# Giving out the last head's second attention pass at the hold point of the stream

## The chip, the cores and the metric

The kernel runs on one core of a Trainium2 chip. The metric is the device time of one execution in microseconds (us). A profile of one execution gives, instruction by instruction, when each engine worked and what it waited for: PE (TensorE, with PEld its weight loads), DVE (VectorE), ACT (ScalarE), POOL (GpSimd) and SP (SyncE, which issues nearly all DMAs here, in order).

## The reference

One layer of a streaming encoder over 2048 positions, 1024 wide, in float32:

```
h   = RMSNorm(x);  z = h @ W_in
A   = gMLP heads:   u * (W_s LN(v) + b), in blocks of 128 positions
B   = 8 FoX heads:  softmax(q k^T / sqrt(64) + c[t] - c[s]) v,  s <= t,
                    c = cumsum(log sigmoid(forget logits))
x   = x + concat(A, B) @ W_out
x   = x + ConvFFN(RMSNorm(x))
out = RMSNorm(x)
```

The change concerns B, the attention, and W_out, which reads A and B.

## The kernel before, in words

Matrix products are made of three matmuls each: operands are split into a rounded high part and the remainder (hi, lo), and mm3 (lines 208, 210 and 212) adds hi hi, hi lo and lo hi. These are the main matmuls; most are 512 wide.

The positions are worked on in two halves of 1024, each of two blocks of 512 (tb = 0 to 3 over both). **Phase A** projects both halves (a_half): gated units, values, keys and queries. **Phase C** (c_half) multiplies the mixed rows by W_out, adds x, and makes the scaled, transposed rows for the ConvFFN. **Phase D** (d_half) is the up-projection of the first half. After it come the second half's C and D and the down-projection.

**The attention stream.** Attention runs beside these phases. b_stream is a generator over 32 pieces (h, tb), in order tb = 0 with heads 0 to 7, then tb = 1, and so on. A piece has two passes. b_max (the first pass) computes the scores of 512 queries against all keys up to them, their running minimum and sums (lines 745 to 754), and from these the row maximum, which a function, turn, transposes on TensorE (line 779) and writes into the tile t1. b_mix (the second pass) recomputes the scores transposed (lines 806 and 807), takes exp (812), splits it into ph and pl (817, 818) and multiplies by the values into the PSUM tile o (794, 795). At a head's end op takes the sum of o's two halves (829, 830); at each odd head op is scaled and split, and written to the DRAM tensors mixh and mixl of that block.

The second pass of a piece is given out after the first pass of the next piece, and that next piece's turn is called inside it, after three of its steps. So todo holds one piece whose second pass is still to come. After every main matmul tick counts, and after each 3.5 to 4.4 of them (RATES) one step of the stream is given out, with priority over the main work. The scheduler then orders each engine's instructions.

**The hold.** The pieces of tb = 2 and 3 need keys and queries of the second half, so b_stream does not begin (0, 2) before ready is set, when phase A has ended; until then it yields without giving anything out. In the kernel's text the stream reaches that point 542 ticks before the end of phase A, with todo = (7, 1).

**Who needs (7, 1).** c_half works on block 0 and then on block 1, each in two column groups of four row tiles. Before the second column group of block 0 it calls need(1), which gives out steps until 16 pieces are done, and then load_mix(1), which reads the mixed rows of block 1 from mixh and mixl into the tiles thi and tlo, in four quarters each (k = 0 to 7 in pairs). The last quarter, k = 6 and 7, holds heads 4 to 7. Each finished row tile is written to rows (DMA rows<-acc), and its buffer acc is loaded anew for block 1 (acc<-in_x_dram); GpSimd makes a scaled copy, ar (line 886), whose eight column blocks TensorE transposes into dn. Weights come through raw (DMA), are rounded by GpSimd (whi, line 150) and split by VectorE (wlo, line 162). In phase D GpSimd also subtracts column blocks of w_down in a tile tw (line 967).

Of the kernel before, what the change touches and what calls it, by code (L numbers as in the profile page):

```python
# [80 lines left out]
class Block:  # L81
# [600 lines left out]
    def b_stream(self, pieces):  # L682

        todo = None
        for h, tb in pieces:
            while tb >= 2 and not self.ready:
                yield
            t1, t2, turn = yield from self.b_max(h, tb)
            if todo:
                yield from self.b_mix(*todo, turn)  # L690
                self.done += 1
            else:
                turn()
            todo = (h, tb, t1, t2, self.rr)
        yield from self.b_mix(*todo, None)
        self.done += 1
# [814 lines left out]
```

## Time and profile before

| | |
|---|---|
| median of 3 timed runs | 2437.68 us (2436.88 to 2441.38) |
| span of the profiled execution | 2436.2 us, 1.5 under that median |
| PE busy | 2409.5 us, 99% |
| DVE, ACT, POOL busy | 1755.8, 1348.5 and 312.5 us |
| phase C begins on PE (first main matmul of c_half) | 592.0 us |
| head 7's second pass over block 1 on PE | 649 to 669 us |

The profile is read as follows. A view of stretches gives busy time by engine and the clock that TensorE was granted (1.00 is full). A timeline gives start, length and the instruction as output<-inputs, and in brackets how long the engine was idle just before and what ended that. Matmul ends are modelled and overlap the next start, so the pace is read from starts. SPq is SyncE's queue: the start of a DMA there is when it was issued, not when it landed.

### The profile page before, as it was taken

To read this page: it belongs to the slowest core of one execution; us is meant where nothing else is said; L and a number is where in the kernel's file an instruction comes from. 1 tells how busy PE (TensorE), PEld (TensorE's weight loads), DVE (VectorE), ACT (ScalarE), POOL (GpSimd) and SP (SyncE) were. 2 spreads that over 40 slices of the span, in tenths; PEclk is the share of its full clock that TensorE was granted. 3 is DMA by queue.
4 is the path that set the end of the run, shared out by engine and by line. 5 is a ranking of instruction groups with operands and counts; after the bars stand their busy time and mean duration, and the time that the engine had idled before them with its cause. 6 is when DMAs were issued, how large, how long until landed. Compare 5 with 4: busy or idle time off the path is not lost.

```text
span 2436.2 us, 32591 instructions
## 1 busy us (share of the span) xinstructions
PE 2409.5 (99%) x10984; PEld 1982.9 (81%) x10984; DVE 1755.8 (72%) x3086; ACT 1348.5 (55%) x2635; POOL 312.5 (13%) x303
## 2 busy tenths in 40 slices
PE   9999999999999999999999999999999999999998
PEld 7788888788777888888888888888888888888887
DVE  5448776565557878878778774498888877957775
ACT  4347766544455556667676671365555555454443
POOL 3114140000213221111111201100000000000000
PEclk9999999999999999999999999999999999999999
DMA  8854646658756545554555436312222228538633
GB/s 290 276 140 123 199 120 174 169 170 280 215 158 213 187 154 164 163 166 144 179 175 180 157 123 236 140 56 80 85 87 87 78 92 311 164 99 297 206 115 121
DMA packets 245031, 400.51 MB, mean 164 GB/s; under 512 B 51240, under 2 KB 109736, under 8 KB 243440
## 3 DMA queue, kind: packets, MB, share of 16 engines
q1 hardware_dynamic: 239824, 374.31, 48.3%
q0 software_dynamic: 5040, 24.12, 2.5%
q8 instruction: 87, 1.43, 0.2%
q14 instruction: 80, 0.66, 0.1%
HBM read 304.76 MB, written 93.72 MB: 164 GB/s over the span
## 4 chain that ended last, share of the span: by engine, by line
PE 93%; DMA 3%; DVE 1%; ACT 1%; issue 0%; POOL 0%; SPq 0%; DVEq 0%; POOLq 0%; ACTq 0%
PE D L1351 16%; PE mm L210 14%; PE mm L208 14%; PE mm L212 14%; PE A L1149 3%; PE A L1150 3%; PE A L1151 3%; PE o L795 2%; PE o L794 2%; PE s L746 2%; PE s L745 2%; PE s L807 2%; PE s L806 2%; PE B L1150 2%; PE B L1151 2%; PE B L1149 2%
## 5 line engine op out<-in xcount | busy, mean ns | idle before, releaser
L210 PE MATMUL mm<-tlo,whi 128*128 128x512 f32 x912 | 358.1, 393 | 0.0
L208 PE MATMUL mm<-thi,whi 128*128 128x512 f32 x912 | 357.7, 392 | 0.0
L212 PE MATMUL mm<-thi,wlo 128*128 128x512 f32 x912 | 357.5, 392 | 0.0
L208 PE MATMUL mm<-whi,thi 128*128 128x512 f32 x640 | 252.9, 396 | 2.9 <-DMA thi<-mixh 2.2
L150 POOL TENSOR_SCALAR whi<-raw 128x1024 fp32r<-128x1024 f32 (+1 forms) x112 | 125.9, 1125 | 1005.1 <-PE mm L210 616.8
L210 PE MATMUL mm<-wlo,thi 128*128 128x512 f32 x640 | 251.3, 393 | 0.1
L212 PE MATMUL mm<-whi,tlo 128*128 128x512 f32 x640 | 251.0, 393 | 0.0
L754 ACT ACTIVATE s<-s,part 128x512 f32<-128x512 f32 (+3 forms) x261 | 154.6, 592 | 130.7 <-DVE part L749 81.4
L208 PEld LDWEIGHTS mm<-thi,whi 128*128 128x128 f32 x912 | 171.5, 188 | 35.7
L210 PEld LDWEIGHTS mm<-tlo,whi 128*128 128x128 f32 x912 | 171.5, 188 | 35.5
L212 PEld LDWEIGHTS mm<-thi,wlo 128*128 128x128 f32 x912 | 171.5, 188 | 34.8
L818 DVE TENSOR_TENSOR pl<-e,ph 128x512 fp32r<-128x512 f32 (+2 forms) x212 | 136.9, 655 | 76.8 <-ACT ph L817 39.3
L162 DVE TENSOR_TENSOR wlo<-raw,whi 128x1024 fp32r<-128x1024 f32 x104 | 136.2, 1309 | 54.0 <-POOL whi L150 53.6
L812 ACT ACTIVATE e<-s 128x512 f32<-128x512 f32 (+2 forms) x216 | 110.3, 527 | 95.3 <-DVE s L810 41.0
L208 PEld LDWEIGHTS mm<-whi,thi 128*128 128x128 f32 x640 | 120.6, 188 | 26.9 <-DMA thi<-mixh 2.5
L1351 PE MATMUL D<-wl,xh 128*128 128x512 f32 x368 | 141.3, 389 | 0.0
L1351 PE MATMUL D<-wh,xh 128*128 128x512 f32 x368 | 140.8, 389 | 0.2 <-DVE xo L1429 0.2
L212 PEld LDWEIGHTS mm<-whi,tlo 128*128 128x128 f32 x640 | 120.3, 188 | 24.3 <-DMA tlo<-mixl 0.7
L210 PEld LDWEIGHTS mm<-wlo,thi 128*128 128x128 f32 x640 | 120.6, 188 | 23.5 <-DVE wlo L162 0.5
L817 ACT ACTIVATE ph<-e 128x512 fp32r<-128x512 f32 (+2 forms) x212 | 116.3, 562 | 39.5 <-PE o L794 34.1
L1351 PE MATMUL D<-wh,xl 128*128 128x512 f32 x368 | 137.1, 389 | 0.0
L749 DVE TENSOR_REDUCE part<-s 128x1 f32<-128x512 f32 x149 | 98.2, 683 | 21.4 <-PE s L746 20.7
(1898 smaller groups left out, 5853.7 us busy)
## 6 DMA issues: line engine op xcount, KB each, us to landing
raw<-in_w_up_dram SPq DMA_DIRECT2D x72, 512.0 KB
m<-kx SPq DMA_DIRECT2D x133, 256.0 KB
m<-kx SPq DMA_DIRECT2D x160, 136.0 KB
x<-act SPq DMA_DIRECT2D x84, 256.0 KB
raw<-in_w_in_dram SPq DMA_DIRECT2D x36, 512.0 KB
v<-vd SPq DMA_DIRECT2D x66, 256.0 KB
raw<-in_w_out_dram SPq DMA_DIRECT2D x24, 512.0 KB
tw<-in_w_down_dram SPq DMA_DIRECT2D x11, 1024.0 KB
```

What stands on the lines that cost most here:

```text
L150: self.cast_ins = self.nc.gpsimd.tensor_scalar(out, in_, 1.0, 0.0, ALU.mult, ALU.add).ins
L162: nc.vector.tensor_tensor(lo, raw, f32(hi), op=ALU.subtract)
L208: mm(ps, lhsT=ah[k], rhs=bh[k], start=k == 0, stop=False)
L210: mm(ps, lhsT=ah[k], rhs=bl[k], start=False, stop=False)
L212: self.last_mm = mm(ps, lhsT=al[k], rhs=bh[k], start=False, stop=k == n - 1).ins
L754: nc.scalar.activation(ps[:, :n], ps[:, :n], AF.Exp, scale=-1.0, bias=dst, accum_out=ls[:, tt, sb:sb + 1])
L817: nc.scalar.activation(ph[:, c], e[:, c], AF.Copy)
L818: nc.vector.tensor_tensor(pl[:, c], e[:, c], f32(ph[:, c]), op=ALU.subtract)
L1149: mm(ps, lhsT=xh[:, ks], rhs=yh[:, k, :], start=fresh and k == 0, stop=False, **kw)
L1150: mm(ps, lhsT=xh[:, ks], rhs=yl[:, k, :], start=False, stop=False, **kw)
L1151: mm(ps, lhsT=xl[:, ks], rhs=yh[:, k, :], start=False, stop=k == 3, **kw)
L1351: nc.tensor.matmul(bank[t], lhsT=x[i][:, ts], rhs=w[k], start=fresh and j == 0 and i + k == 0, stop=last and i == 1, **kw)
```

## The change

When the stream comes to a piece that is held back, it now gives out the second pass of the piece before at once, with no turn in it (None), counts it as done and empties todo. Then it waits as before. The held piece's own turn is later called directly after its first pass, as for the stream's first piece.

```
         todo = None
         for h, tb in pieces:
-            while tb >= 2 and not self.ready:
-                yield
+            if tb >= 2 and not self.ready:
+                if todo:
+                    yield from self.b_mix(*todo, None)
+                    self.done += 1
+                    todo = None
+                while not self.ready:
+                    yield
             t1, t2, turn = yield from self.b_max(h, tb)
             if todo:
                 yield from self.b_mix(*todo, turn)
```

Lines behind it are numbered five higher in the changed kernel (794 becomes 799, 806 becomes 811). It also changes what stands on the engines, from the place where head 6's second pass over block 1 ends. Here is TensorE there, in the kernel before: o is head 6's output, mm main work of phase C, and lines 745 and 746 head 0's first pass over block 2.

```order
L795 MATMUL o_1160_4894<-pl_1201_5033,v_1187_4984 128x256
L794 MATMUL o_1160_4894<-ph_1204_5048,v_1187_4984 128x128
L208 MATMUL mm_1443_6373<-whi_1432_6350,thi_1321_5823 128x512
L745 MATMUL s_1359_6022<-m1_53_394,t1_55_396 128x512
L745 MATMUL s_1360_6032<-m1_53_394,t1_55_396 128x512
L745 MATMUL s_1361_6041<-m1_53_394,t1_55_396 128x512
L746 MATMUL s_1359_6022<-m2_1358_6019,t2_1354_6012 128x512
L795 MATMUL o_1160_4894<-pl_1205_5049,v_1187_4984 128x128
```

The same place on TensorE in the changed kernel; lines 811 and 812 are head 7's second pass over block 1.

```order
L799 MATMUL o_1160_4894<-ph_1200_5032,v_1187_4984 128x256
L811 MATMUL s_1210_5077<-t1_54_395,m1_53_394 128x512
L811 MATMUL s_1214_5090<-t1_54_395,m1_53_394 128x512
L811 MATMUL s_1220_5109<-t1_54_395,m1_53_394 128x512
L812 MATMUL s_1214_5090<-t2_1124_4764,m2_1208_5072 128x512
L812 MATMUL s_1210_5077<-t2_1124_4764,m2_1208_5072 128x512
L800 MATMUL o_1160_4894<-pl_1201_5033,v_1187_4984 128x256
L799 MATMUL o_1160_4894<-ph_1204_5048,v_1187_4984 128x128
```

Head 7's second pass now stands where head 0's first pass over block 2 stood, and the latter comes behind it.

SyncE's queue of DMAs, where head 7's result is written (mixh1, mixl1) and the last quarter of block 1 read (thi_1428, tlo_1430), before; qx, kx and vd are queries, keys and values of the stream.

```order
L100 DMA v_1473_6525<-vd0_77 128x4x128
L100 DMA v_1492_6590<-vd0_77 128x4x128
L100 DMA m1_52_393<-kx1_74 68x512
L100 DMA m2_1457_6457<-kx1_74 128x512
L100 DMA mixh1_80<-ph_1420_6317 128x512
L100 DMA thi_1428_6338<-mixh1_80 128x2x512
L100 DMA mixl1_84<-pl_1421_6318 128x512
L100 DMA m1_53_394<-kx0_73 68x512
L100 DMA m2_1472_6522<-kx0_73 128x512
L100 DMA tlo_1430_6340<-mixl1_84 128x2x512
```

The same in the changed kernel (the tiles are thi_1439 and tlo_1441 there).

```order
L100 DMA acc_1563_6795<-in_x_dram 128x1024
L100 DMA v_1487_6540<-vd0_77 128x4x128
L100 DMA m1_53_394<-kx1_74 68x512
L100 DMA m2_1410_6222<-kx1_74 128x512
L100 DMA rows0_3_90<-acc_1381_6102 128x1024
L100 DMA mixh1_80<-ph_1250_5240 128x512
L100 DMA mixl1_84<-pl_1251_5241 128x512
L100 DMA acc_1564_6797<-in_x_dram 128x1024
L100 DMA thi_1439_6389<-mixh1_80 128x2x512
L100 DMA tlo_1441_6391<-mixl1_84 128x2x512
```

Write and read moved forward, in among the last of the four writes of row tiles (rows0) and the loads of acc for block 1; before, all of these stood ahead of them.

GpSimd at the start of phase D before, where ar_1705 is the scaled copy of the last row tile of block 1.

```order
L175 TENSOR_SCALAR rs_1707_7436<-ss_1706_7434 128x1
L150 TENSOR_SCALAR whi_1731_7464<-raw_1730_7463 128x1024
L177 TENSOR_TENSOR rstd_1708_7438<-rs_1707_7436,mhalf_63 128x1
L886 TENSOR_SCALAR ar_1705_7433<-acc_1547_6735,rstd_1708_7438 128x1024
L967 TENSOR_TENSOR tw_1839_7920<-tw_1839_7920 128x512 x2
L150 TENSOR_SCALAR whi_1935_8330<-raw_1934_8329 128x1024
L967 TENSOR_TENSOR tw_1839_7920<-tw_1839_7920 128x512 x2
```

And in the changed kernel, where the same copy is ar_1746.

```order
L972 TENSOR_TENSOR tw_1880_8035<-tw_1880_8035 128x512 x2
L175 TENSOR_SCALAR rs_1748_7548<-ss_1747_7546 128x1
L972 TENSOR_TENSOR tw_1880_8035<-tw_1880_8035 128x512
L177 TENSOR_TENSOR rstd_1749_7550<-rs_1748_7548,mhalf_63 128x1
L150 TENSOR_SCALAR whi_1976_8445<-raw_1975_8444 128x1024
L972 TENSOR_TENSOR tw_1880_8035<-tw_1880_8035 128x512
L891 TENSOR_SCALAR ar_1746_7545<-acc_1564_6797,rstd_1749_7550 128x1024
```

The copy moved from ahead of the four subtractions in tw to behind them.

## Prediction, made before the result was known

> **What bounds the kernel now.** First the page's head and its busy times.
>
> ```profile
> span 2436.2 us, 32591 instructions
> PE 2409.5 (99%) x10984; PEld 1982.9 (81%) x10984; DVE 1755.8 (72%) x3086; ACT 1348.5 (55%) x2635; POOL 312.5 (13%) x303
> ```
>
> TensorE is busy for all but 26.7 us. The change neither adds nor drops an instruction that computes, so only two things can move: TensorE's idle time and the time for which its clock is low. The second view cuts the span into stretches: length, busy time and instructions of PE, PEld, DVE, ACT, POOL, then the granted clock.
>
> ```profile
> 630.00:663.00 33.00, 33.00 (x158) 27.32 (x157) 17.09 (x39) 19.04 (x45) 7.43 (x12) 1.00 0.66 204
> 663.00:670.00 7.00, 4.75 (x31) 3.70 (x29) 4.84 (x10) 4.25 (x10) 0.00 (x0) 1.00 0.56 156
> 670.00:675.00 5.00, 3.29 (x16) 2.18 (x16) 4.87 (x9) 4.55 (x12) 0.00 (x0) 1.00 0.44 130
> 675.00:682.00 7.00, 3.91 (x9) 2.28 (x10) 3.77 (x9) 3.91 (x13) 0.00 (x0) 0.55 0.64 184
> 682.00:686.00 4.00, 4.00 (x11) 2.72 (x10) 1.38 (x4) 0.67 (x2) 0.00 (x0) 0.51 0.56 180
> 686.00:700.00 14.00, 14.00 (x62) 11.49 (x63) 7.52 (x17) 7.66 (x16) 1.06 (x1) 1.00 0.18 58
> 800.00:1560.00 760.00, 759.17 (x3447) 627.20 (x3446) 569.62 (x1105) 472.18 (x1022) 129.10 (x121) 1.00 0.51 168
> ```
>
> One hole stands out: 2.25 + 1.71 + 3.09 = 7.05 us idle between 663 and 682, and a granted clock of 0.55 and 0.51 from 675 to 686. The long stretch behind 800 idles for 0.8 us in all. So the third view is TensorE's timeline through the hole (start, length, what; in brackets the idle time just before and what ended it).
>
> ```profile
> 663.63 0.60 PE L183 MATMUL s<-ident,rw 128*128 128x128 f32 x4
> ...
> 668.76 0.27 PE L795 MATMUL o<-pl,v 128*128 128x128 f32 x1
> 670.19 0.50 PE L745 MATMUL s<-m,t 96*128 96x512 f32 x1 [1.15 <-ACT s L754]
> 670.53 0.40 PE L746 MATMUL s<-m,t 128*128 128x512 f32 x1
> 670.77 1.03 PE L183 MATMUL dn<-ident,ar 128*128 128x128 f32 x8
> 671.56 0.50 PE L745 MATMUL s<-m,t 96*128 96x512 f32 x1
> ...
> 678.89 0.42 PE L746 MATMUL s<-m,t 128*128 128x256 f32 x1
> 681.53 0.79 PE L208 MATMUL mm<-whi,thi 128*128 128x512 f32 x1 [2.22 <-DMA thi<-mixh]
> 682.12 0.63 PE L210 MATMUL mm<-wlo,thi 128*128 128x512 f32 x1
> ...
> 685.92 0.50 PE L212 MATMUL mm<-whi,tlo 128*128 128x512 f32 x1
> ```
>
> Until 681.53 there is no main matmul in it, only the stream's scores and transposes, each waiting for ScalarE or a load; then the main matmul waits for thi<-mixh, the last quarter of block 1's mixed tile. The chain that ended last says why it is late.
>
> ```profile
> 670.16 0.59 ACT op L829
> 673.34 0.53 ACT ph L196
> 673.88 3.30 DMA mixh<-ph
> 677.20 4.28 DMA thi<-mixh
> 681.53 0.79 PE mm L208
> ```
>
> Head 7's second pass over block 1 ends on TensorE at 668.76 (row above); its scaling, its write to mixh and the read back take 12.8 us more. Phase C's first half-block has used up its own work by then.
>
> **The change part by part.** *What the hole costs.* In full flow a 512-wide matmul issues every 2.72 / 12 = 0.227 us, by these rows from before the hole, 12 steps apart.
>
> ```profile
> 595.21 0.39 PE L212 MATMUL mm<-whi,tlo 128*128 128x512 f32 x1
> ...
> 597.93 0.39 PE L807 MATMUL s<-t,m 128*128 128x512 f32 x1
> ```
>
> Narrower ones cost their share, and a transpose 0.10 (eight from 670.77 to 671.56). From 663.63 to 685.92, 22.3 us, TensorE issues 26 matmuls 512 wide, four each of 384, 256 and 128, and 20 transposes: 5.90 + 0.68 + 0.45 + 0.23 + 2.0 = 9.3 us of work. The hole costs 13.0 us: 7.05 idle, about 4 from the half clock (10 matmuls worth 2.15 us from 681.53 to 685.92 take 4.39; six worth 0.79 from 676.30 to 679.31 take 2.7 without their wait), and the rest in refilling the array after each wait.
>
> *What goes.* In the new order head 7's second pass follows head 6's directly, at 619.3 us, where head 0's first pass over block 2 stood. Up to there TensorE's rows are the same. From there to the first matmul that needs the last quarter the new order has 170 matmuls 512 wide, 19 narrower and 12 transposes; the old order's first 170 wide ones, 15 narrower and 17 transposes took from 619.33 to 663.63. So TensorE asks for the quarter at about 663.6, not having to pass 18 wide stream matmuls first, if nothing new holds it.
>
> *When the quarter is there.* Head 7's last o matmul now stands at about 650, some 19 us earlier, so its ph, 5.1 us later (668.76 to 673.88 in the rows above), is ready near 655. The pass's loads of keys and values move with it on SyncE's queue, past head 0's t loads; these come later, but head 0's first score stands 17 us later on TensorE too, and that hides it. But SyncE's queue is in order, and the write now stands behind the fourth rows<-acc, the read behind the fourth acc load, each of which waits for the rows write before it:
>
> ```profile
> 633.24 0.38 SPq L100 DMA_DIRECT2D rows<-acc  x1
> 639.52 0.33 SPq L100 DMA_DIRECT2D acc<-in_x_dram  x1
> ...
> 652.28 0.42 SPq L100 DMA_DIRECT2D rows<-acc  x1
> 657.91 0.33 SPq L100 DMA_DIRECT2D acc<-in_x_dram  x1
> ```
>
> Four rounds take 24.7 us, 5.3 to 6.3 each. They start after the first column group, which ends where it did, so the read goes out at about 658.7 and lands 4.3 later, at 663.0. That is a tie with TensorE: 0.5 us of wait, between 0 and 6 (four rounds of 7.5).
>
> *What is new at 620 to 635.* The second pass of head 7 needs VectorE at once: mask, pl, and op to free the o bank. VectorE is held there by a weight split:
>
> ```profile
> 627.25 1.23 DVE L162 TENSOR_TENSOR wlo<-raw,whi 128x1024 fp32r<-128x1024 f32 x1 [6.56 <-POOL whi L150]
> ...
> 630.19 0.67 DVE L830 TENSOR_TENSOR op<-o,op 64x512 f32<-64x512 f32 x1
> ```
>
> In the new order two pl and another split stand between them, so op ends near 632.6, and the first o matmul wants the bank, and the last two scores theirs behind the masks, from about 631.6. I take 2 us, between 0 and 4. Head 0's turn is now called without a second pass around it; by the order it stands some 6 us behind head 0's last score, beside other work: nothing, at most 1.
>
> *What is late next.* Phase C ends about 20 us earlier: 13 from the hole and the rest because about 10 us of stream work now follows it. At the start of phase D TensorE transposes the four scaled rows; GpSimd makes the last one, ar.
>
> ```profile
> 742.29 1.65 POOL L886 TENSOR_SCALAR ar<-acc,rstd 128x1024 f32<-128x1024 f32 x1
> 743.90 2.99 POOL L967 TENSOR_TENSOR tw<-tw 128x512 f32<-128x512 f32 x2
> 746.86 1.49 POOL L150 TENSOR_SCALAR whi<-raw 128x1024 fp32r<-128x1024 f32 x1
> 748.32 3.93 POOL L967 TENSOR_TENSOR tw<-tw 128x512 f32<-128x512 f32 x2
> ```
>
> ```profile
> 744.00 0.33 PE L183 MATMUL dn<-ident,ar 128*128 128x128 f32 x1
> ```
>
> TensorE met it at 744.00, just as it was done. In the new order ar stands behind the four tw subtractions and that cast, 8.3 us of GpSimd's time (743.90 to 752.25), and TensorE wants it near 727 (744.0 less 13.0, less 6.1 us of stream work that now comes after, plus the 2.5 above). The cast's and tw's loads are asked for earlier too, since they wait for weight buffers that TensorE frees. I take 1.5 us of wait, between 0 and 5. The stream then runs 11 steps ahead in phase D, which idles for 0.8 us in 760 today: 0, within 1.
>
> *The sum.* -13.0 + 0.5 + 2 + 1.5 = -9.0 us. The span is 2436.2 and the median of the timed runs 2437.7, so I add 1.5 for what lies around it: 2436.2 - 9.0 + 1.5 = 2428.7, say 2429. Ends of this case: -13.0 - 1 gives 2424, and +6, +4 and +5 do not come together; two of them give about 2434.
>
> *The clock.* The rows show the clock at half while no single wait was over 2.22 us, in a stretch 37% idle (7.05 of 19 us); so I let the 4 us go with the hole. The Trainium skill, "TensorE: Matmul & The Clock Gate", section "HAM oscillation — how this bites in real kernels", gives the rule as no idle gaps over about 3.4 us. This trace does not agree: shorter gaps, close together, went with the low clock.
>
> **The rivals.** *The ring keeps it* (0.13). The quarter's read goes out behind rounds of 8 us: it lands about 7 us later than reckoned, TensorE waits 7 us, and the clock falls for a further 2. Then -13.0 + 7 + 2 + 2 + 1.5 = -0.5: 2437. For it: the rounds wait for DMA, which TensorE's pace does not hasten. Against it: the four rounds that the trace shows at this very place.
>
> *The low clock is not the hole's doing* (0.07). If only a long single gap can lower the clock, the 4 us stay wherever the clock's window falls, and -9.0 + 4.1 = -4.9: 2433. Against it: 1.00 on both sides of the hole. By the rule of the page named above, the Trainium skill's, the gaps were too short, and this case's sum would hold.
>
> *GpSimd becomes the bound* (0.05), the slower side. If ar at the start of phase D is set by SyncE's chain of rows, acc, raw and tw, which does not move, then it comes 8.3 us after today's 743.9, at 752. TensorE's work would bring it there at 727.4; 25 us of wait undo the gain and cost about 14 more: 2452. It decides from an ar later than about 743: 738 eats the gain, 4.9 more make it slower. Against it: that chain's start moves forward with the rows that TensorE finishes.
>
> *It does not do what it says* (0.05): the scheduler moves the pass but other waits of the stream, bank or key loads, take all back: 2437 to 2438.
>
> **How the numbers follow.** The forecast holds 0.70. About 0.2% of the time, 4.9 us, is what a measurement can tell from no change. Faster takes the forecast and the edge of the clock case, 0.72; the same takes the ring, the rest of the clock case, the last rival and a few high ends, 0.22; slower 0.06. The range for 8 in 10 goes from 2424 to 2436: the forecast's own ends, 2424 to 2434, and on to the lower part of the cases without a gain.
>
> **What would show it.** Right: no wait for thi<-mixh above 2 us near 663, a granted clock of 1.00 throughout 663 to 700, mixh<-ph issued near 655 and not at 673.88, and phase C's last matmul some 20 us earlier. The new waits are on o (L799) and s (L811) near 632 and on dn near 727. Wrong: the fourth thi<-mixh issued after 664, a low clock anywhere in 660 to 760, or a wait of over 5 us for ar.

## The result, and the profile after

| | before | after |
|---|---|---|
| median of the timed runs, same chip | 2439.09 us (4 runs) | 2425.27 us (2424.89 to 2425.82, 4 runs) |
| ratio, 95% interval | | 0.9944 [0.9932, 0.9956] |
| profiled span | 2436.2 us | 2423.6 us |

Faster by 12.6 us in the span and 13.8 in the medians; forecast was 9.0. The medians and ratios in this document leave out two runs that were far slower than the rest of their kernel, one of e_turn (6031.59 us) and one of e_late40 (4038.61 us). On a second chip (run c_after below) the ratio was 0.9958 [0.9946, 0.9971]. The page's head shows TensorE's idle time falling from 26.7 to 19.6 us.

```profile
span 2423.6 us, 32604 instructions
PE 2404.0 (99%) x10984; PEld 1981.1 (82%) x10984; DVE 1755.0 (72%) x3086; ACT 1352.4 (56%) x2635; POOL 315.8 (13%) x303
```

So 7.1 of the 12.6 us are idle time; the rest must be work that runs faster. The stretches of the changed kernel show both (length, busy time of PE, PEld, DVE, ACT, POOL, then the granted clock):

```profile
630.00:663.00 33.00, 32.48 (x153) 26.58 (x152) 17.00 (x30) 17.34 (x39) 8.02 (x12) 1.00 0.82 250
663.00:670.00 7.00, 5.94 (x33) 4.78 (x32) 3.96 (x10) 2.58 (x8) 0.00 (x0) 1.00 0.49 159
670.00:675.00 5.00, 5.00 (x24) 4.12 (x23) 2.97 (x11) 1.74 (x5) 0.00 (x0) 1.00 0.27 82
675.00:682.00 7.00, 7.00 (x37) 5.72 (x36) 5.11 (x7) 2.82 (x6) 2.50 (x2) 1.00 0.01 2
682.00:686.00 4.00, 4.00 (x23) 3.33 (x22) 3.53 (x5) 2.16 (x5) 1.05 (x2) 1.00 0.73 177
...
720.00:740.00 20.00, 19.42 (x95) 15.49 (x94) 15.70 (x30) 11.47 (x24) 6.93 (x7) 1.00 0.73 232
740.00:760.00 20.00, 20.00 (x100) 16.58 (x99) 13.06 (x28) 11.83 (x29) 0.93 (x1) 1.00 0.30 83
800.00:1560.00 760.00, 758.98 (x3448) 626.85 (x3447) 570.22 (x1101) 475.92 (x1036) 129.84 (x124) 1.00 0.52 169
```

From 663 to 686 the idle time is 1.06 us where it was 7.05, and the clock is full throughout. In those 23 us TensorE starts 109 matmuls; before it started 63. SyncE's queue shows why (start of each DMA's issue):

```profile
650.54 0.33 SPq L100 DMA_DIRECT2D acc<-in_x_dram  x1
654.36 0.32 SPq L100 DMA_DIRECT2D rows<-acc  x1
654.77 0.38 SPq L100 DMA_DIRECT2D mixh<-ph  x1
655.55 0.41 SPq L100 DMA_DIRECT2D mixl<-pl  x1
659.04 0.33 SPq L100 DMA_DIRECT2D acc<-in_x_dram  x1
659.67 0.37 SPq L100 DMA_DIRECT2D thi<-mixh  x1
660.67 0.37 SPq L100 DMA_DIRECT2D tlo<-mixl  x1
```

The write goes out at 654.77 (673.88 before), the read of the last quarter at 659.67 (677.20 before). In TensorE's timeline every wait from 630 to 670 that ended on another engine or a DMA is one of these two:

```profile
632.85 0.50 PE L799 MATMUL o<-ph,v 128*128 128x512 f32 x1 [0.52 <-DVE op L835]
666.89 0.50 PE L212 MATMUL mm<-whi,tlo 128*128 128x512 f32 x1 [1.06 <-DMA tlo<-mixl]
```

**Where it came from.** Two marks cut the span: TensorE's first main matmul of phase D and its last main matmul, at the end of the second half's phase C (the down-projection comes behind it, on other lines). Before:

```profile
734.15 0.39 PE L208 MATMUL mm<-thi,whi 128*128 128x512 f32 x1
...
1580.86 0.39 PE L212 MATMUL mm<-whi,tlo 128*128 128x512 f32 x1
```

After:

```profile
713.20 0.39 PE L208 MATMUL mm<-thi,whi 128*128 128x512 f32 x1
...
1568.98 0.39 PE L212 MATMUL mm<-whi,tlo 128*128 128x512 f32 x1
```

Phase D starts 20.95 us earlier, the last main matmul comes 11.88 earlier, the end 12.6. The 9.1 us between the first two figures are mostly stream work that now runs behind the mark and not ahead of it; they are no loss. Up to the mark TensorE had 3420 matmuls before and has 3368 now; 38 of those 52 are 512 wide, 8.6 us at 0.227 each.

### The profile page after: what moved, and what is told of

Its sections match the earlier page's. It is cut to its first block, busy times and chain, and to the rows that moved or that the text cites. A ratio compares the mean times of both kernels' runs of the same rounds, so it can differ in the third digit from the quotient of the medians.

```text
span 2423.6 us, 32604 instructions
## 1 busy us (share of the span) xinstructions
PE 2404.0 (99%) x10984; PEld 1981.1 (82%) x10984; DVE 1755.0 (72%) x3086; ACT 1352.4 (56%) x2635; POOL 315.8 (13%) x303
## 4 chain that ended last, share of the span: by engine, by line
PE 68%; DMA 2%; DVE 2%; ACT 1%; issue 1%; POOL 0%; SPq 0%; DVEq 0%; POOLq 0%; ACTq 0%
PE D L1356 14%; PE mm L212 8%; PE mm L208 8%; PE mm L210 8%; PE A L1154 3%; PE A L1156 3%; PE A L1155 3%; PE o L800 2%; PE o L799 2%; PE B L1156 2%; PE B L1155 2%; PE B L1154 2%; PE s L751 1%; PE s L750 1%; PE s L812 1%; PE s L811 1%
## 5 line engine op out<-in xcount | busy, mean ns | idle before, releaser
L823 DVE TENSOR_TENSOR pl<-e,ph 128x512 fp32r<-128x512 f32 (+1 forms) x218 | 146.6, 681 | 76.0 <-ACT ph L822 42.4
L817 ACT ACTIVATE e<-s 128x512 f32<-128x512 f32 (+1 forms) x222 | 113.8, 529 | 109.5 <-DVE s L815 49.5
L822 ACT ACTIVATE ph<-e 128x512 fp32r<-128x512 f32 (+1 forms) x218 | 120.1, 563 | 43.6 <-PE o L799 41.1
```

The source lines that it names most:

```text
L822: nc.scalar.activation(ph[:, c], e[:, c], AF.Copy)
L823: nc.vector.tensor_tensor(pl[:, c], e[:, c], f32(ph[:, c]), op=ALU.subtract)
```

## The experiments

**Theory 1**: the gain is the earlier arrival of block 1's last quarter, and nothing else. **Rivals**: the head's turn outside the second pass is what helps; the stream's other order or its lead of 11 steps in later phases is what helps. A separate question is whether the low clock in the hole followed from the idle time. Marks below are as above; "beside it" is the kernel before, on the same chip.

**e_turn: one part of the change alone.**

```
+                if (h, tb) == (0, 2):
+                    turn()
+                    turn = None
                 yield from self.b_mix(*todo, turn)
```

> The kernel before, with one part of the change alone: head 0's own turn (block 2) is called directly after its first pass, and head 7's second pass over block 1 then runs behind it without a turn inside. The passes stay in their old order. Theory 1 (the gain is the earlier arrival of block 1's last quarter): head 7's last o stays near 669, thi<-mixh is waited for near 681 as before, the clock falls there, and the time stays within 1 us of before (2438 to 2440). Rival (part of the gain is that the turn no longer stands inside the second pass and holds up its o matmuls): 3 to 6 us less than before, 2433 to 2436, with the wait for thi<-mixh shorter by as much.

2439.40 us against 2438.61 beside it, ratio 1.0004 [0.9994, 1.0013]. Its stretches at the hole:

```profile
675.00:682.00 7.00, 3.68 (x10) 2.12 (x9) 3.21 (x8) 3.82 (x12) 0.00 (x0) 0.57 0.61 168
682.00:686.00 4.00, 3.95 (x10) 2.75 (x10) 1.71 (x7) 1.03 (x3) 0.00 (x0) 0.50 0.57 168
```

The hole stays with its low clock; the write goes out at 673.30. The turn by itself is worth nothing, as theory 1 has it.

**e_late16 and e_late40: the changed order, with the quarter held back.** Added for head 7 of block 1 only, ahead of the write (40 in the second):

```
+        if (h, tb) == (7, 1):
+            for _ in range(16):
+                nc.gpsimd.tensor_scalar(oh, f32(oh), 1.0, 0.0, ALU.mult, ALU.add)
```

> The changed kernel, with the write of block 1's last rows to the DRAM tensor held back: 16 multiplications by one in GpSimd over head 7's rounded output, one after the other, some 0.5 to 0.6 us each, together about 9 us. Nothing else of the stream waits for it. Theory 1: mixh<-ph goes out near 663 in place of 654.8, the last quarter lands near 672, TensorE asks for it near 670 (main work of the next half-block cannot pass it, some stream work can): a wait of 1 to 5 us comes back, and the time is 1 to 5 us over the changed kernel's. Rival (the gain is from the stream's other order or from its being 11 steps ahead later): within 1 us of the changed kernel.

> As the run with 16 multiplications, with 40, together about 22 us: the last quarter of block 1 then lands near 685, later than in the kernel before (681.5), while the order of the stream's passes stays the changed one. Theory 1: the hole comes back, 4 to 10 us of wait, and with it (if idle time does it) a clock near half for some us: 5 to 13 us over the changed kernel, so that the most of the gain of 14 is gone. Rival (the other order of the stream is what gains): at most 2 us over the changed kernel.

With 16: 2442.16 us, ratio 1.0015 [1.0005, 1.0024]; span 2437.3, that is 13.7 over the changed kernel. With 40: 2445.51, ratio 1.0034 [1.0020, 1.0048]; span 2444.2. The whole gain is gone, and more. SyncE's queue and TensorE with 16:

```profile
668.88 0.32 SPq L100 DMA_DIRECT2D mixh<-ph  x1
672.80 0.37 SPq L100 DMA_DIRECT2D thi<-mixh  x1
```

```profile
676.62 0.80 PE L208 MATMUL mm<-whi,thi 128*128 128x512 f32 x1 [4.04 <-DMA thi<-mixh]
```

Direction as theory 1 says, size well beyond it: I had reckoned 0.55 us for a multiplication. GpSimd's timeline of the run with 16:

```profile
659.12 9.73 POOL L849 TENSOR_SCALAR ph<-ph 128x512 fp32r<-128x512 f32 x14
```

That is 0.70 each, with other work of GpSimd between the first ones, so the write went out 14.1 us later (668.88 less 654.77), not 9, and with 40 it went out at 687.02, 32.3 later. Of the 13.7 us with 16, some 4.5 are more idle time from 660 to 680 (5.60 against 1.06), 4.4 more idle time from 800 to 1560 (5.38 against 1.02), and the clock was low for 6.8 us. The stretch in phase D with 16:

```profile
800.00:1560.00 760.00, 754.62 (x3420) 620.93 (x3419) 572.59 (x1104) 477.00 (x1034) 127.39 (x119) 1.00 0.51 166
```

So about 9 of the 13.7 us belong to the late quarter itself, and the rest is lost later. The scheduler also moved some things around the held write: mixl, its read and some key loads now go ahead of it on SyncE's queue, so the arrival is not the only difference. The rival's "within 1 or 2 us" is refuted all the same: same passes in the changed order, same lead, late quarter, no gain.

**e_order: the changed order of the two passes, given out only when phase A has ended.**

```
             while tb >= 2 and not self.ready:
                 yield
+            if (h, tb) == (0, 2):
+                yield from self.b_mix(*todo, None)
+                self.done += 1
+                todo = None
```

> The kernel before, with head 7's second pass over block 1 given out in front of head 0's first pass over block 2, but only when phase A has ended in the kernel's text (not at the hold point, 542 ticks before). The order of the two passes is that of the change; when they are given out is that of before, so the stream is not ahead in the later text. Theory 1 (only that the pass stands in front of head 0's first pass, so that the last quarter is there in time): the hole is gone, 2424 to 2427. Rival (being given out at the hold point itself matters, since the pass can then fill waits of phase A or put the stream ahead): at least 3 us less gained, 2428 or more.

2435.73 us, ratio 0.9987 [0.9978, 0.9996]: only some 3 us of the gain. This I had not expected. Its stretches:

```profile
660.00:680.00 20.00, 18.21 (x92) 14.78 (x91) 10.91 (x27) 7.63 (x19) 0.37 (x1) 1.00 0.36 123
...
800.00:1560.00 760.00, 754.32 (x3418) 620.88 (x3417) 566.64 (x1099) 473.34 (x1031) 129.77 (x120) 1.00 0.51 168
```

The hole is gone, with full clock, and phase D starts at 713.64, 0.4 us behind the changed kernel. The loss is behind that mark: 5.68 us idle from 800 to 1560 against 1.02, and the last main matmul at 1576.11 against 1568.98. TensorE's longest wait there, and VectorE just before it:

```profile
1015.01 0.70 PE L810 MATMUL dn<-t,m 128*128 128x512 f32 x2 [2.75 <-ACT s L758]
```

```profile
1004.87 2.30 DVE L162 TENSOR_TENSOR wlo<-raw,whi 128x1024 fp32r<-128x1024 f32 x1 [2.21 <-POOL whi L150]
1007.10 0.68 DVE L753 TENSOR_REDUCE part<-s 128x1 f32<-128x512 f32 x1
```

A weight split holds up the stream's minima, with other work of VectorE and ScalarE in between, then ScalarE's sums, then the bank of the next scores. The other waits there are for key loads (m<-kx, 2.4 us in three) and for pl (0.6). In the kernel's text the difference is this: the changed kernel uses 11 of the stream's steps that are given out empty at the hold point in e_order and before. So its stream ends with main matmul 3855, where that of before ends with 3888 and that of e_order with 3895.

**e_slow: the changed kernel, lead taken back.** RATES[2] from 4.4 to 4.8.

> The changed kernel, with phase D's rate of the stream at one step in 4.8 main matmuls in place of 4.4, which gives back the lead that the stream has there in the changed kernel. Theory 1: the lead is worth nothing, so the time is within 1.5 us of the changed kernel's. Rival (the lead takes waits out of phases C and D and is part of the gain, as the wait of 1.7 us at 748 to 753 that went): 2 to 5 us over the changed kernel.

I named the rate wrongly: RATES[2] holds during phase C of the first half, not phase D. So the lead was down from 11 steps to 4 by the time phase D ran. 2432.28 us, ratio 0.9977 [0.9968, 0.9985]; phase D starts at 711.89, and then:

```profile
800.00:1560.00 760.00, 756.27 (x3425) 623.30 (x3424) 557.06 (x1100) 475.55 (x1032) 127.36 (x120) 1.00 0.52 168
```

3.73 us idle. The median is 2.8 us over that of the changed kernel on this chip (c_after, below), in the rival's band, though single runs of the two overlap. Two kernels now put part of the gain on the lead, so it was tested in its own right, with the changed kernel beside it.

**c_after, e_lead, c_before: the lead given to e_order.** e_lead is e_order with

```
-        self.rate = RATES[3]
+        self.rate = 3.0
+        self.defer(198, lambda: setattr(self, "rate", RATES[3]))
```

> The changed kernel itself, unaltered, measured again beside the next two. The order-alone run reached phase D as early as the changed kernel (713.6 and 713.2 us) and lost 7 us behind it, where it waits for key loads; the run with the slower rate reached it at 711.9 and lost 4 to 5. If these waits are a matter of the execution (loads that take longer on some chips or days): this run shows them as well, 2429 to 2434. If the lead of the stream is what keeps them away: 2424 to 2427 here too, with at most 1.5 us idle on TensorE from 800 to 1560.

> The order-alone kernel with the missing lead given back in phase D: one step of the stream per 3.0 main matmuls in place of 3.6 over the first 198 of them, after which the stream is 11 steps ahead and ends with the same main matmul as in the changed kernel. If the lead is worth the 7 us: within 1.5 us of the changed kernel beside it. If the waits there are a matter of the execution, or of something else in the order: within 2 us of the order-alone kernel, 2434 to 2437.

> The kernel before itself, unaltered, for a second profile on this chip. If waits for loads in phase D vary from execution to execution: its idle time on TensorE from 800 to 1560 is not the 0.8 us of the first profile but 2 us or more. If they come only with the other order or the lead: 0.8 again, within 0.5.

c_after: 2429.44 us, ratio 0.9958 [0.9946, 0.9971]. e_lead: 2427.70, ratio 0.9955 [0.9941, 0.9968]. All 10 runs of e_order on this chip are at 2431.34 or over, and all 5 of each of these two at 2430.86 or under. c_before, one profile: span 2435.8, and 0.3 us idle from 800 to 1560. e_lead there:

```profile
800.00:1560.00 760.00, 760.00 (x3452) 627.71 (x3451) 568.45 (x1101) 477.01 (x1037) 131.04 (x124) 1.00 0.52 169
```

So the lead, and not the chip or the day, keeps these waits away in the profiles. With the hole filled, the 11 steps of lead decide about 5.7 us of idle time (5.68 against 0.00) and the refilling behind it: 2435.73 against 2427.70 in the medians. c_after's median missed its band by 2.4 us upward, into the band of the other reading, while its idle time of 0.81 us was as forecast. Each of these kernels has one profile only, so what makes other executions longer isn't known; this chip's runs of the changed kernel spread over 6.7 us (2424.20 to 2430.86) where the first chip's spread over 0.9.

**b_lead and e_lead22: the lead without the order, and twice the lead.** b_lead is the kernel before with e_lead's edit, e_lead22 is e_lead with 2.57 for 3.0.

> The kernel before, with the lead alone: one step of the stream per 3.0 main matmuls in place of 3.6 over the first 198 of phase D. Order of the passes and hole stay as before. If the lead is a gain by itself (slack against loads): 4 to 8 us less than before, 2431 to 2434. If it only decides how the stream's steps meet the main work's weight splits in phase D, where the kernel before idles for 0.3 to 0.8 us already: within 2 us of before, 2436 to 2440, with the hole unchanged.

> The order-alone kernel with twice the lead: one step per 2.57 main matmuls over the first 198 of phase D, so that the stream is 22 steps ahead. If the lead is slack against late loads: no more than 1.5 us over the run with 11 steps (2427.7), or under it. If what counts is where the steps fall against the weight splits and loads of the main work: the waits in phase D come back in part, 2430 to 2436.

b_lead: 2440.94 us, ratio 1.0009 [1.0000, 1.0018]: nothing gained, if anything 1 to 2 us lost, and the hole is there (wait for thi 3.4 us). e_lead22: 2428.64, ratio 0.9953 [0.9939, 0.9966], the same as with 11 steps. The lead is worth nothing while the hole stands and some 8 us once it is gone; more of it brings nothing more. Nor does the lead alone keep the waits away: e_late16 has all 11 steps, a hole, and 5.38 us idle in phase D. So theory 1 falls in its second half: the early quarter removes the hole, and of the time that this frees only some 3 us stay without the lead. Whether it works as slack against late operands, or by moving the stream's minima away from the weight splits, these runs don't tell: b_lead and e_late16 speak for the second, e_lead22 for the first.

**e_acc5: a fifth buffer for acc in the changed kernel.**

> The changed kernel, with a fifth buffer for acc, so that the loads of the next half-block's acc need not all wait for the rows' writes ahead of them on SyncE's queue. If the ring of rows and acc still sets when the last quarter's write and read go out (mixh<-ph at 654.8, the last o at 650.5): they go out some us earlier, the 1.1 us wait for tlo goes, and the time is 0.5 to 1.5 us under the changed kernel's. If it is head 7's own chain that sets it: within 0.5 us.

2430.69 us, ratio 0.9973 [0.9962, 0.9984], against 2429.44 of c_after on the same chip: no gain, 1.3 us over and so in neither band. SyncE's queue:

```profile
649.70 0.38 SPq L100 DMA_DIRECT2D rows<-acc  x1
655.56 0.33 SPq L100 DMA_DIRECT2D acc<-in_x_dram  x1
655.98 0.38 SPq L100 DMA_DIRECT2D mixh<-ph  x1
656.42 0.42 SPq L100 DMA_DIRECT2D mixl<-pl  x1
```

Head 7's last matmul for o ran at 649.53 and its ph was ready at 653.33, but the write stands behind the third acc load, which waits for its row's write. So here the ring sets the time of the write, one round earlier in the order and no earlier on the clock (654.77 in the changed kernel, though phase C began 1.9 us later in this run, at 594.04); the wait for thi was 2.5 us. In the changed kernel it did not: ph was ready at 654.50, 0.27 us before its write went out. No version tried beats the changed kernel beyond what the runs can tell.

**e_busy: does the clock follow the idle time?** The kernel before, with the score pairs of head 0's first pass issued twice:

```
+                for _ in range(2 if (h, tb) == (1, 2) else 1):
-                nc.tensor.matmul(ps[:, :n], lhsT=t1[0:96, ts], rhs=m1[0:96, :n], start=True, stop=False)
-                nc.tensor.matmul(ps[:, :n], lhsT=t2[:, ts], rhs=m2[:, :n], start=False, stop=True)
+                    nc.tensor.matmul(ps[:, :n], lhsT=t1[0:96, ts], rhs=m1[0:96, :n], start=True, stop=False)
+                    nc.tensor.matmul(ps[:, :n], lhsT=t2[:, ts], rhs=m2[:, :n], start=False, stop=True)
```

> The kernel before, with each score pair of head 0's first pass over block 2 issued twice into the same bank (the second pair overwrites the first, the result is the same): 12 more pairs, at most 24 x 0.227 = 5.4 us more TensorE work, which lies in or beside the hole from 663 to 686. The last quarter comes as late as before. If the low clock follows the share of idle time in a stretch (the prediction's reading): busy time in 663 to 682 rises, the clock stays at 0.8 to 1.0 in 675 to 686, its some 4 us come back, and the extra work costs 1 to 5 us beyond what the waits hide: -3 to +2 us against before. If single waits or something else set the clock: it stays near 0.5 from 675 to 686 and the time is 0 to +5 us against before.

(The expectation says head 0; in the edit the piece (1, 2) is head 1's first pass over block 2, the one that stands in the hole.) 2441.69 us, ratio 1.0013 [1.0003, 1.0022], 3.1 us more than beside it; phase D starts at 735.13, between the two profiles of before (734.15, and 735.48 in c_before). Its stretches:

```profile
676.00:679.00 3.00, 2.80 (x12) 1.77 (x12) 2.13 (x4) 2.30 (x7) 0.00 (x0) 1.00 0.59 210
679.00:682.00 3.00, 0.86 (x7) 0.65 (x6) 1.16 (x5) 1.69 (x6) 0.00 (x0) 1.00 0.64 204
682.00:685.00 3.00, 2.57 (x7) 2.19 (x8) 0.00 (x0) 0.00 (x0) 0.00 (x0) 0.54 0.69 255
685.00:688.00 3.00, 3.00 (x14) 2.54 (x13) 1.70 (x6) 1.00 (x3) 0.00 (x0) 0.89 0.13 42
```

The wait at the end of the hole:

```profile
682.43 0.80 PE L208 MATMUL mm<-whi,thi 128*128 128x512 f32 x1 [2.58 <-DMA thi<-mixh]
```

From 663 to 679 TensorE was idle for 1.32 us, and for 4.84 before. The clock now stays full until 682.2 and is low for 3.4 us, where it was low for 10.2 (675.7 to 685.9) in the first profile of before and for 6.8 in c_before. So the clock moved with the idle time, as expected; but it still fell, after the wait of 2.58 us, and this run alone doesn't tell the share of idle time from that single wait (the last section does). The time is outside what I had for this reading (-3 to +2) and inside the other's (0 to +5): up to phase D the second pairs cost what the clock and the waits gave back, and the 3 us came behind it, where nothing was changed; the cause is open.

## Why the prediction was right, and where its sum was off

**The hole and its cause: right.** The quarter's arrival was the bound. e_late16 and e_late40 keep the changed order, hold back the arrival and lose the gain, about 9 of the 13.7 us of e_late16 at that place; e_order sets the order alone and the hole goes. That the time so freed stays free to the end was the step that I didn't examine (the rest of D, below). Its price of 13.0 us fits: 5.99 us less idle time from 663 to 686, about 4 from the clock, the rest refilling, of which little is left.

**When the quarter is there: right, on the other half.** The write was forecast near 655 and went out at 654.77; the read at 658.7 and went out at 659.67. TensorE waits 1.06 us, 0.5 forecast, for tlo and not for thi. The chain that ended last in the changed kernel has this before that wait:

```profile
654.92 0.61 DVE pl L197
655.55 5.05 DMA mixl<-pl
660.67 6.18 DMA tlo<-mixl
```

So the low half decided, by way of VectorE's pl and two DMAs, while I had reckoned with the high half alone: ph ready near 655, and a read that lands after 4.3 us. The read of thi did go out behind the fourth acc load (659.04), as forecast. The ring rival (0.13) did not come true. From a rows write to the next acc load the four rounds took 4.3, 6.4, 4.8 and 4.7 us, where the trace of before had 5.3 to 6.3. The fourth write of rows went out only at 654.36, because VectorE had its row ready only at 654.33, not because of a DMA.

**New waits at 620 to 635: right place, too dear.** The wait on op is there, 0.52 us at 632.85. Op ended at 632.79, as forecast (632.6), but TensorE came for the bank at 632.33 and not at 631.6, and no score waited behind a mask. From 620 to 640 TensorE was idle for 1.24 us, and for 1.00 before: 0.24 more, not 2. A wait also went that I didn't take off: before, head 0's first score had waited 0.32 us for its queries at 621.44. The wait for a rounded weight (0.67 us at 627.27, now 0.65 at 627.81) is in both.

**ar behind GpSimd's tw work: this term failed.** I took 1.5 us; it is 0. GpSimd's and TensorE's timelines in the changed kernel:

```profile
722.95 1.28 POOL L972 TENSOR_TENSOR tw<-tw 128x512 f32<-128x512 f32 x1
724.22 2.08 POOL L891 TENSOR_SCALAR ar<-acc,rstd 128x1024 f32<-128x1024 f32 x1
```

```profile
725.71 0.49 PE L183 MATMUL dn<-ident,ar 128*128 128x128 f32 x3
727.23 0.38 PE L183 MATMUL dn<-ident,ar 128*128 128x128 f32 x2
```

The order was as I read it, ar last; but the work ahead of it began at 715.75, 28 us earlier than before (743.90), and ended at 724.23, so ar was done at 726.30 and wanted at 727.23. TensorE came when I said, near 727; the margin is 0.93 us. The loads ahead of GpSimd moved forward with the buffers that TensorE frees, which I had in the text and not in the sum.

**The rest of D: the number right by luck.** I said 0, within 1, and from 800 to 1560 the idle time changed from 0.83 to 1.02 us. But the reason, that phase D idles so little today, doesn't carry: e_order keeps the stream's old steps and loses 4.9 us there. The change brings its own remedy, the 11 steps, which I put at nothing. Nor did I see that the waits for pl at 740 to 760 would go. Before:

```profile
740.00:760.00 20.00, 18.29 (x85) 13.58 (x83) 18.05 (x24) 11.63 (x21) 12.12 (x9) 1.00 0.81 275
```

That is 1.71 us less idle time, with 0.58 more at 720 to 740 for a query load (t<-qx, at 735.52).

**The sum.** -13.0 + 1.06 + 0.24 + 0 - 1.71 + 0.58 = -12.8 against -12.6 measured; forecast -9.0. The 13.0 in it is the forecast's own figure, which no run measured by itself. The difference of 3.6 is made of the ar term (1.5), the waits at 620 to 635 (1.8) and those for pl (1.7), less 0.6 each for tlo and the query load; these five give 3.8. The median of 2425.27 is in the range, near its lower end.

**The clock rival** (0.07) is out: no stretch of the changed kernel from 600 to 760 shows less than 1.00. **GpSimd as the bound** (0.05) is out by the rows above, and **it does not do what it says** (0.05) is out because the hole went.

## What to carry to other kernels

Where a side stream feeds the main work at a few points, look not for the engine that is busiest but for the last producer that the main work waits for, and put it ahead of side work that nobody waits for; the test is to hold that result back by itself, as e_late16 does. A filled hole moves everything behind it closer to its operands, so a later phase that idles for nothing today can begin to wait: measure the change with and without the slack that it happens to bring. Price new waits as a difference from the waits that stood at that place before.

## What the runs showed of the hardware

The clock fell without a long wait. With 40 multiplications the wait just before the fall was 1.45 us, the longest of that stretch; then TensorE was busy for 92% of the time or more, at half clock (the run's stretches):

```profile
673.00:676.00 3.00, 1.55 (x8) 0.76 (x6) 3.00 (x7) 2.56 (x7) 2.66 (x5) 1.00 0.00 0
676.00:679.00 3.00, 2.95 (x8) 1.62 (x6) 2.10 (x4) 2.35 (x8) 2.59 (x5) 0.52 0.47 135
...
682.00:685.00 3.00, 2.77 (x7) 1.63 (x7) 1.98 (x8) 2.05 (x7) 2.67 (x5) 0.50 0.35 109
```

The longest single wait does not decide: e_acc5 waited 2.54 us in one piece (up to 665.41) and kept the full clock, longer than any wait before the falls in before (1.15) and e_late40 (1.45). Read in slices of 0.2 us, the clock was low for 3.4 us in e_busy, 6.8 in e_late16 and c_before, 10.2 in before, e_turn and e_late40 (there for another 3.4 from 693.2), and in b_lead once for 3.4 and once for 6.8: one, two and three times 3.4. That fits the window of about 3.4 us that runs freely, as the Trainium skill has it in "TensorE: Matmul & The Clock Gate", section "What's actually happening". The rule of gaps over about 3.4 us on that page of the Trainium skill ("HAM oscillation — how this bites in real kernels") does not agree with this kernel, where idle time made of gaps of 0.2 to 1.5 us was enough. Which share decides was not settled: the changed kernel and e_order had 1.06 and 1.46 us idle within 3 us (664 to 667) and kept the full clock.
